# Two MLPs of a decoder trunk: up projections with activations held in the array, seven block products for eight in three of eight chunk pairs, and one written order for all engines

## The chip, the cores and the metric

The kernel runs on one core of one Trainium2 chip. Its metric is device microseconds of one execution; the number given for a kernel is the median over its runs. The engines of a core are named as in the profile: PE is the matrix engine (PEld its weight loads), DVE the vector engine, ACT the scalar engine, POOL and SP the two others. SP's queue issues the loads of weights.

## The reference, cut to what matters

D is 2048, there are 256 tokens (two blocks of 128, called b = 0 and 1 below), the hidden width of an MLP is 8192, and everything is float32.

```python
def sq_relu_mlp(u, w_up, w_down):
    return jnp.square(jax.nn.relu(u @ w_up)) @ w_down
...
    for i in range(DEPTH):
        u = rmsnorm(h, mix_pre_g[i])
        if i < N_A:
            m = short_conv_mixer(u, a_w_in[i], a_conv_w[i], a_w_out[i])
        else:
            j = i - N_A
            m = stick_breaking_mixer(u, b_w_q[j], k_sh, v_sh, b_w_o[j])
        h = h + rmsnorm(m, mix_post_g[i])
        u = rmsnorm(h, mlp_pre_g[i])
        h = h + rmsnorm(sq_relu_mlp(u, mlp_w_up[i], mlp_w_down[i]), mlp_post_g[i])
        if i == N_A - 1:
            kv = rmsnorm(h, kv_norm_g) @ w_kv
```

Layer 0 mixes with a gated convolution (a 2048 x 6144 and a 2048 x 2048 projection), layer 1 with causal stick-breaking attention over 16 heads (projections k, q, v and o of 2048 x 2048 each). Both layers end in an MLP of 2048 x 8192 and 8192 x 2048.

## The kernel before

**Numbers in two parts.** Each float32 operand is split into a high part (ACT copies it to the type fp32r, line 148) and a low part (DVE subtracts the high part, line 151). A product of two operands is three matmuls: high x high, high x low, low x high. Activations are split once; each weight is split once, in chunks of 128 x 1024 that SP loads into a ring of 4 buffers (`RAW`); the two parts go to a ring of 7 (`RING`).

**Stages, in order.** The projection into the convolution (lines 423 and 425), the projection out of it, the MLP of layer 0, the stage of k, q and v with the attention between them, the projection o, the MLP of layer 1.

**An MLP.** The hidden width is cut into four quarters of 2048. Each quarter is an up stage and then a down stage.
- *Up* (`up`, lines 550 and 557; 552 at the start of a layer): for each 128 x 128 tile of the weight, the tile is the held operand, and the activations stream past it: one matmul of 512 columns (the high tile against the high and the low part of 256 tokens) and one of 256 columns (the low tile against the high part). Eight tiles of a column go together. The result comes out transposed, features on the partitions, which is how the down stage wants it. `hidden` (lines 530 to 533) adds the two halves, applies the squared ReLU on DVE, and `split_tile` (176, 177) splits it.
- *Down* (`Group.half`, lines 224 to 226): the activations are the held operand, 128 x 128, and 512 columns of the weight stream: three matmuls of 512 columns, which I call a product. A quarter has two groups (`project`), one for each half of the 2048 output columns; a group has 16 chunks, and each chunk two token blocks and two halves of 512 columns: 64 products. Its four results, (b, c), are in four PSUM banks. Down results of the quarters are summed in SBUF (line 593).

**Norms.** `Norms.post` and `finish` (lines 301 to 334) take the last results of a stage, form the residual h, multiply it by the row of gains, and `enter` has PE transpose it (line 182), ACT and DVE split it (189, 190). At such a seam the last four chunks are done block by block (`EDGE`), so that block 0 is normalised while PE works on block 1.

**Who sets the order.** PE's order is written by hand. That of the other engines comes from the framework's scheduler, with some instructions marked as urgent, and small steps of the attention and the norms are put off by delays in a clock that counts PE's work (`at`, `spent`). h lives in SBUF throughout.

Of the kernel before, what the change touches and what calls it, by code (L numbers as in the profile page):

```python
# [2 lines left out]

# [12 lines left out]
P = 128  # L16
# [12 lines left out]
LEAD_UP = 6  # L29
ALONE = 8  # L30
RING = 7
RAW = 4
AHEAD = 4
CALM = 12
UNIT = 1.36
TURNS = (4.7, 6.8, 10.5, 13.0)
SQUARES = 20.0
TILE_HIGH = 0.227
TILE_LOW = 0.12
FIRST = 2  # L40
QUARTERS = FF // D

IN_N = [j * KD + i for i in range(KD) for j in range(3)]


def lead_then_rows(ns, lead):

    return [(k, n) for k in range(KD) for n in ns[:lead]] + [(k, n) for n in ns[lead:] for k in range(KD)]


IN_ORDER = lead_then_rows(IN_N, LEAD)
UP_FIRST = lead_then_rows(list(range(KD)), LEAD_UP)
UP_ORDER = lead_then_rows(list(range(KD)), 0)

G_MIX0, G_KV, G_MIX1, G_C0, G_C1, G_C2 = range(6)
B_POST0, B_MLP0, B_MPOST0, B_POST1, B_MLP1, B_MPOST1 = range(6)
# [3 lines left out]
def trunk(ctx, tc, x, xT, vecs, rows, ws, out):  # L60
    nc = tc.nc
    ctx.enter_context(tc.manual_schedule(engines={mybir.EngineType.PE}))
    const = ctx.enter_context(tc.tile_pool(name="const", bufs=1))
    stat = ctx.enter_context(tc.tile_pool(name="stat", bufs=8))
    res = ctx.enter_context(tc.tile_pool(name="res", bufs=8))
    act = ctx.enter_context(tc.tile_pool(name="act", bufs=8))
    wpool = ctx.enter_context(tc.tile_pool(name="w", bufs=RAW))
    wsplit = ctx.enter_context(tc.tile_pool(name="ws", bufs=RING))
    psum = ctx.enter_context(tc.tile_pool(name="ps", bufs=1, space=bass.MemoryType.PSUM))

    gv = const.tile([P, 6, KD], F32, name="gv")
    nc.scalar.dma_start(gv[:], vecs.rearrange("p (g k) -> p g k", g=6))

    def g(i, k):
        return gv[:, i, k : k + 1]

    eps = const.tile([P, 1], F32, name="eps")
    nc.vector.memset(eps[:], EPS)
    mean = const.tile([P, P], F32, name="mean")
    nc.vector.memset(mean[:], 1.0 / D)  # L80
    ones = const.tile([P, P], F32, name="ones")
    nc.vector.memset(ones[:], 1.0)

    def selected(name, pattern, op, multiplier):
        t = const.tile([P, P], F32, name=name)
        nc.gpsimd.affine_select(
            out=t[:], in_=ones[:], pattern=[[pattern, P]], compare_op=op,
            fill=0.0, base=0, channel_multiplier=multiplier,
        )
        return t  # L90

    later = selected("later", -1, ALU.is_gt, 1)
    causal = selected("causal", 1, ALU.is_gt, -1)
    ident = selected("ident", 1, ALU.is_equal, -1)
    later_r = const.tile([P, P], F32R, name="later_r")
    nc.vector.tensor_copy(later_r[:], later[:])
    ones_r = const.tile([P, P], F32R, name="ones_r")
    nc.vector.tensor_copy(ones_r[:], ones[:])
    nc.scalar.preload_act_table_set("sqrt_and_others")

    def bank(i, name):
        return psum.tile([P, 512], F32, tag=f"b{i}", name=name)


    stream = []

    class Weights:


        def __init__(self, ap, gains=None):  # L110
            self.ap, self.gains = ap, gains
            self.base = len(stream)
            stream.extend((self, c) for c in range(ap.shape[0]))

    raw, parts = {}, {}
    last_load = [None]
    count = {"loaded": 0, "split": 0, "limit": 1 << 30}
    gate = []

    def behind(kind):  # L120
        return tc.issue_after(gate[kind].ins) if gate else nullcontext()

    def load_one():
        i = count["loaded"]
        if i >= len(stream):
            return
        w, c = stream[i]
        t = wpool.tile([P, CW], F32, tag="raw", name=f"raw{i}")
        n = HALF if i < FIRST else CW
        for a in range(0, CW, n):  # L130
            last_load[0] = nc.sync.dma_start(t[:, a : a + n], w.ap[c, :, a : a + n])
        raw[i] = t
        count["loaded"] += 1

    def split_one():
        i = count["split"]
        while count["loaded"] <= i:
            load_one()
        w, c = stream[i]
        t = raw.pop(i)  # L140
        hi = wsplit.tile([P, CW], F32R, tag="hi", name=f"whi{i}")
        lo = wsplit.tile([P, CW], F32R, tag="lo", name=f"wlo{i}")
        gains = w.gains(c) if w.gains else [None] * (4 if i < FIRST else 1)
        n = CW // len(gains)
        for j, gain in enumerate(gains):
            at = slice(j * n, (j + 1) * n)
            with behind(0):
                nc.scalar.activation(hi[:, at], t[:, at], AF.Copy, scale=1.0 if gain is None else gain)  # L148
            with behind(1):
                if gain is None:  # L150
                    nc.vector.tensor_tensor(lo[:, at], t[:, at], hi[:, at].bitcast(F32), op=ALU.subtract)  # L151
                else:
                    nc.vector.scalar_tensor_tensor(  # L153
                        lo[:, at], t[:, at], gain, hi[:, at].bitcast(F32), op0=ALU.mult, op1=ALU.subtract
                    )
        parts[i] = hi, lo
        count["split"] += 1
        load_one()

    def chunk(i):  # L160
        while count["split"] <= min(i + (AHEAD if i >= CALM else 2), len(stream) - 1, max(i, count["limit"])):
            split_one()
        return parts[i]


    def operand(name):
        return act.tile([P, 4, 2, NB, P], F32R, tag="x4", name=name)

    def part_of(xs, k, b, i):
        return xs[k // 4][:, k % 4, i, b, :]  # L170

    def split_tile(xs, k, src):

        hi, lo = xs[k // 4][:, k % 4, 0, :, :], xs[k // 4][:, k % 4, 1, :, :]
        src = src.rearrange("p (b t) -> p b t", b=NB)
        nc.scalar.activation(hi, src, AF.Copy)
        nc.vector.tensor_tensor(lo, src, hi.bitcast(F32), op=ALU.subtract)

    def transposed(src, to):

        for j in range(4):
            nc.tensor.transpose(to[:, j * P : (j + 1) * P], src[:, j * P : (j + 1) * P], ident[:])  # L182
        return to[:].rearrange("p (k t) -> p k t", k=4)

    def operand_from(src, x4, b, to):
        t = transposed(src, to)
        hi, lo = x4[:, :, 0, b, :], x4[:, :, 1, b, :]
        return (
            nc.scalar.activation(hi, t, AF.Copy),
            nc.vector.tensor_tensor(lo, t, hi.bitcast(F32), op=ALU.subtract),  # L190
        )


    clock = {"us": 0.0, "seq": 0}
    due = []

    def at(delay, fn):
# [47 lines left out]
    def run(groups, enter=False, leave=False):  # L245
# [6 lines left out]
        for gr, i in units[first:last]:  # L252
            if i == 0 and gr.start is not None:
                gr.start()
            for b in range(NB):
                gr.unit(b, i)
# [595 lines left out]
```

## Time and profile before

| what | |
|---|---|
| median of 3 runs (lowest, highest) | 2197.94 us (2196.91, 2198.6) |
| the profiled execution: span from first to last instruction | 2195.9 us, 2.0 under the median |
| PE busy | 2171.5 us, 99% of the span, 11058 matmuls |
| DVE busy | 1334.1 us, 61% |
| ACT busy | 1115.9 us, 51% |
| moved by DMA | 417 MB, mean 190 GB/s |

The page's span is the profiled execution's own time as far as the profile shows it; what lies around it is the difference to the runs' times, some 2 us. A group of instructions is given as a line with its count, then busy time and the mean duration of one in ns, then the idle time of its engine just before its instructions and who ended it. Mean durations overlap on one engine: the next instruction often starts before the one ahead has ended, so what an instruction costs in a dense stretch is the distance between starts, which the timeline shows.

### The profile page before, as it was taken

To read this page: it belongs to the slowest core of one execution; us is meant where nothing else is said; L and a number is where in the kernel's file an instruction comes from. 1 tells how busy PE (TensorE), PEld (TensorE's weight loads), DVE (VectorE), ACT (ScalarE), POOL (GpSimd) and SP (SyncE) were. 2 spreads that over 40 slices of the span, in tenths; PEclk is the share of its full clock that TensorE was granted. 3 is DMA by queue.
4 is the path that set the end of the run, shared out by engine and by line. 5 is a ranking of instruction groups with operands and counts; after the bars stand their busy time and mean duration, and the time that the engine had idled before them with its cause. 6 is when DMAs were issued, how large, how long until landed. Compare 5 with 4: busy or idle time off the path is not lost.

```text
span 2195.9 us, 28873 instructions
## 1 busy us (share of the span) xinstructions
PE 2171.5 (99%) x11058; PEld 1852.0 (84%) x11058; DVE 1334.1 (61%) x1830; ACT 1115.9 (51%) x1534; POOL 4.3 (0%) x13
## 2 busy tenths in 40 slices
PE   8999999999999999999999999999999999999998
PEld 7888888888888888888788888879888888888886
DVE  7766656754654664565656777467545645655655
ACT  7544445544443443444557887455445434544443
POOL 0000000000000000000000000000000000000000
PEclk9999999999999999999999999999999999999999
DMA  8666565666656656655565556556666666666663
GB/s 304 205 191 188 188 229 163 211 190 193 193 185 195 193 185 193 194 188 180 175 201 163 157 160 195 188 173 203 189 193 192 186 194 195 187 189 198 186 190 115
DMA packets 114618, 417.16 MB, mean 190 GB/s; under 512 B 12849, under 2 KB 12849, under 8 KB 113457
## 3 DMA queue, kind: packets, MB, share of 16 engines
q1 hardware_dynamic: 112896, 407.95, 58.8%
q0 software_dynamic: 864, 6.29, 0.8%
q8 instruction: 86, 1.41, 0.2%
q10 hardware_dynamic: 720, 1.10, 0.1%
q14 instruction: 52, 0.42, 0.1%
HBM read 413.19 MB, written 2.10 MB: 189 GB/s over the span
## 4 chain that ended last, share of the span: by engine, by line
PE 97%; DVE 2%; ACT 0%; issue 0%; DMA 0%; DVEq 0%; ACTq 0%
PE up L550 20%; PE acc L224 17%; PE acc L226 17%; PE acc L225 17%; PE up L557 11%; PE acc L423 7%; PE acc L425 4%; PE lead L423 1%; DVE h L324 1%; PE tr L182 1%; PE up L552 1%; PE lead L425 1%; DVE hg L334 0%; PE z L645 0%; PE o L693 0%
## 5 line engine op out<-in xcount | busy, mean ns | idle before, releaser
L151 DVE TENSOR_TENSOR wlo<-raw,whi 128x1024 fp32r<-128x1024 f32 (+1 forms) x678 | 822.0, 1215 | 714.0 <-ACT whi L148 703.4
L148 ACT ACTIVATE whi<-raw 128x1024 fp32r<-128x1024 f32 (+1 forms) x678 | 712.5, 1053 | 932.3 <-PE acc L226 448.0
L550 PE MATMUL up<-u,whi 128*128 128x512 f32 x1952 | 489.4, 392 | 0.0
L550 PEld LDWEIGHTS up<-u,whi 128*128 128x128 f32 x1952 | 351.2, 189 | 62.8
L224 PE MATMUL acc<-whi,hid 128*128 128x512 f32 x1024 | 398.5, 389 | 0.0
L225 PE MATMUL acc<-wlo,hid 128*128 128x512 f32 x1024 | 398.4, 389 | 0.0
L226 PE MATMUL acc<-whi,hid 128*128 128x512 f32 x1024 | 398.4, 389 | 0.0
L557 PEld LDWEIGHTS up<-u,wlo 128*128 128x128 f32 x2048 | 278.6, 190 | 19.4
L557 PE MATMUL up<-u,wlo 128*128 128x256 f32 x2048 | 285.1, 282 | 0.0
L226 PEld LDWEIGHTS acc<-whi,hid 128*128 128x128 f32 x1024 | 192.3, 188 | 40.0
L224 PEld LDWEIGHTS acc<-whi,hid 128*128 128x128 f32 x1024 | 192.3, 188 | 39.6
L225 PEld LDWEIGHTS acc<-wlo,hid 128*128 128x128 f32 x1024 | 192.3, 188 | 39.4
L423 PE MATMUL acc<-u,whi 128*128 128x512 f32 x672 | 168.4, 392 | 0.0
L153 DVE SCALAR_TENSOR_TENSOR wlo<-raw,gv,whi 128x512 fp32r<-128x512 f32 (+1 forms) x160 | 132.2, 853 | 54.5 <-ACT whi L148 53.8
L224 PE MATMUL acc<-whi,u 128*128 128x512 f32 x384 | 153.2, 399 | 0.1
L226 PE MATMUL acc<-whi,u 128*128 128x512 f32 x384 | 150.0, 391 | 1.5 <-DVE u L190 1.5
L148 ACT ACTIVATE whi<-raw,gv 128x512 fp32r<-128x512 f32 (+1 forms) x160 | 121.9, 801 | 56.3 <-PE acc L226 49.7
L225 PE MATMUL acc<-wlo,u 128*128 128x512 f32 x384 | 149.7, 390 | 0.0
L423 PEld LDWEIGHTS acc<-u,whi 128*128 128x128 f32 x672 | 120.9, 189 | 21.6
L425 PEld LDWEIGHTS acc<-u,wlo 128*128 128x128 f32 x672 | 91.7, 190 | 6.6
L425 PE MATMUL acc<-u,wlo 128*128 128x256 f32 x672 | 93.7, 282 | 0.0
L226 PEld LDWEIGHTS acc<-whi,u 128*128 128x128 f32 x384 | 72.1, 188 | 17.5 <-DVE u L190 2.0
(133 smaller groups left out, 1607.4 us busy)
## 6 DMA issues: line engine op xcount, KB each, us to landing
raw<-w_up SPq DMA_DIRECT2D x256, 512.0 KB, 3.7
raw<-w_dn SPq DMA_DIRECT2D x256, 512.0 KB, 3.6
raw<-w_in SPq DMA_DIRECT2D x94, 512.0 KB, 4.4
raw<-w_out SPq DMA_DIRECT2D x32, 512.0 KB, 3.8
raw<-w_v SPq DMA_DIRECT2D x32, 512.0 KB, 4.3
raw<-w_k SPq DMA_DIRECT2D x32, 512.0 KB, 4.2
raw<-w_q SPq DMA_DIRECT2D x32, 512.0 KB, 3.9
raw<-w_wo SPq DMA_DIRECT2D x32, 512.0 KB, 4.3
```

Of the source, the lines that this page charges most:

```text
L148: nc.scalar.activation(hi[:, at], t[:, at], AF.Copy, scale=1.0 if gain is None else gain)
L151: nc.vector.tensor_tensor(lo[:, at], t[:, at], hi[:, at].bitcast(F32), op=ALU.subtract)
L153: nc.vector.scalar_tensor_tensor(lo[:, at], t[:, at], gain, hi[:, at].bitcast(F32), op0=ALU.mult, op1=ALU.subtract)
L182: nc.tensor.transpose(to[:, j * P : (j + 1) * P], src[:, j * P : (j + 1) * P], ident[:])
L224: nc.tensor.matmul(ps[:], xh, hi[:, a], start=i == 0 and k == 0, stop=False)
L225: nc.tensor.matmul(ps[:], xh, lo[:, a], start=False, stop=False)
L226: nc.tensor.matmul(ps[:], xl, hi[:, a], start=False, stop=i == self.n - 1 and k == self.ks - 1)
L324: nc.vector.scalar_tensor_tensor(piece(h[b], c), self.mg[b][c], r[:], piece(h[b], c), op0=ALU.mult, op1=ALU.add)
L423: nc.tensor.matmul(ps[:], w, xs, start=k == 0, stop=False)
L425: nc.tensor.matmul(ps[:, :T], w, xs[:, :T], start=False, stop=k == KD - 1)
L550: nc.tensor.matmul(ps, weight(0, k, n), x, start=k == 0, stop=False)
L557: nc.tensor.matmul(pss[n][:, :T], weight(1, k, n), x, start=False, stop=k == KD - 1)
```

## The change

Most of the file is written anew; the stages, the split into high and low parts and the chunks of 128 x 1024 stay. (Tile names: ru, hu, lu are a chunk of an up weight as loaded, its high and its low part, rd, hd, ld the same of a down weight; the digits are layer, quarter, group, chunk, or with a letter a to d the four operands of a seven.)

1. **Up with activations held.** Up stages now use the same three matmuls of 512 columns as the down stages (`product`, line 560): two groups of 64 products in a quarter. The result has tokens on the partitions, so each 128 x 512 result is evicted, transposed by PE in four 128 x 128 pieces, passed through ReLU and square on ACT, and split (`up_evict`). Before, hidden results needed no transposes.

2. **Seven products for eight.** A pair of chunks is a 2 x 2 block matrix of the weight (two k blocks, two halves of 512 columns) and meets a 2 x 2 block matrix of activations (two token blocks, two k blocks): eight products. In 14 of the 16 groups of an MLP, three of the eight pairs (`UP_SEVEN`, `DN_SEVEN`) take seven products of sums instead (`Group.seven`): DVE makes four sums of weight blocks of 512 columns (t1 to t4), which yields three and a half chunks to split in place of two; four sums of activation blocks are made once per operand (`make_forms`). Three of the seven products go into the accumulators of the group, four into banks q1, q5, q6 and q7, added up over the three pairs. After the third one, `combine` makes four sums of these on ACT and DVE, and the eviction adds one of them to each accumulator on DVE. The two groups without sevens are the first up and the last down group of an MLP. The order of pairs in a group is 3, 0, 4, 1, 5, 2, 6, 7, where 0, 1 and 2 are the sevens.

3. **One written order for all engines.** Nothing is left to the framework's scheduler. Every instruction is a task with a duration, buffers, PSUM banks and a due time; `Plan.place` walks through a model of the engines at build time, and the order that comes out is issued on all of them. Rings are now `SLOTS`: 8 for loaded chunks, 6 for high and 6 for low parts.

4. **Smaller.** Down results of quarters 1 to 3 start from the sum so far, which ACT copies into the PSUM bank (`seeds`). h goes to DRAM (`hs`) and comes back for the next norm. The gains ahead of an MLP are applied per feature during the split behind the transposes, no longer as a row.

```diff
-RING = 7
-RAW = 4
...
+SLOTS = {"raw": 8, "r2": 2, "hi": 6, "lo": 6, "x8": 8, "x4": 6, "c2": 14}
...
+UP_SEVEN = (0, 1, 2)
+DN_SEVEN = (0, 1, 2)
...
-                nc.tensor.matmul(ps, weight(0, k, n), x, start=k == 0, stop=False)
...
-                nc.tensor.matmul(pss[n][:, :T], weight(1, k, n), x, start=False, stop=k == KD - 1)
...
+    def product(ps, xh, xl, hi, lo, first, last, skip):
+        def fn():
+            for j, (a, w) in enumerate(((xh, hi), (xh, lo), (xl, hi))):
+                nc.tensor.matmul(
+                    ps.w(), a.w(), w.w(), start=first and j == 0, stop=last and j == 2, skip_group_check=skip
+                )
...
+        def seven(self, j, last):
...
+            b11, b22, b21, b12 = r0.col(0, HALF), r0.col(HALF, CW), r1.col(0, HALF), r1.col(HALF, CW)
+            t1, t2, t3, t4 = r2.col(0, HALF), r2.col(HALF, CW), b12, r3.col()
...
+                tt(t1, b12, b11, ALU.add)
+                tt(t3, b12, b22, ALU.add)
+            tt(t2, t1, b22, ALU.add)
+            tt(t4, t2, b21, ALU.add)
...
+            x2 = split(r2, f"{self.name}{j}c")
+            prod(q(5), "q5", s("s1"), x2, 0)
+            prod(q(6), "q6", s("s2"), x2, 1)
+            x0 = split(r0, f"{self.name}{j}a")
+            prod(q(1), "q1", a(0, 0), x0, 0)
+            prod(self.acc(0, 1).col(), (0, 1), s("s4"), x0, 1)
+            x1 = split(r1, f"{self.name}{j}b")
+            prod(q(7), "q7", s("s3"), x1, 1)
+            prod(self.acc(0, 0).col(), (0, 0), a(0, 1), x1, 0)
+            x3 = split(r3, f"{self.name}{j}d", 0, HALF)
+            prod(self.acc(1, 0).col(), (1, 0), a(1, 1), x3, 0)
...
+        def combine(self):
...
+            act(q1, q[1].col(), AF.Copy, soon=1.0)
+            tt(v, q[6].col(), q1, ALU.subtract, soon=2.0)
+            tt(v5, v, q[5].col(), ALU.add, soon=3.0)
+            tt(v, v, q[7].col(), ALU.add, soon=4.0)
+            tt(w5, v, q[5].col(), ALU.add, soon=5.0)
...
+                        st = add
+                        tt(st, ps, add, op, soon=1.5)
+                    tr = bank(banks[b][c], "tr")
+                    transposed(tr, st)
...
+                        act(r.col(), tr.col(), AF.Relu, soon=4.0)
+                        act(r.col(), r.col(), AF.Square, soon=8.0)
...
+                    act(piece(hid, n, 0, b), src, AF.Copy, soon=9.0)
+                    tt(piece(hid, n, 1, b), src, piece(hid, n, 0, b), ALU.subtract, soon=10.0)
```

**The order at three places.** All are in layer 0, third quarter. First PE in the second half of the up stage. Before, this is one column of 16 tiles (whi272 and whi273 are the high parts of two chunks, u4 the activations).

```order
L550 MATMUL up_6869<-u4_3416,whi272_6766 128x512 x4
L550 MATMUL up_6869<-u4_3477,whi272_6766 128x512 x4
L557 MATMUL up_6869<-u4_3416,wlo272_6767 128x256 x4
L557 MATMUL up_6869<-u4_3477,wlo272_6767 128x256 x4
L550 MATMUL up_6869<-u4_3547,whi273_6788 128x512 x4
L550 MATMUL up_6869<-u4_3589,whi273_6788 128x512 x4
L557 MATMUL up_6869<-u4_3547,wlo273_6789 128x256 x4
L557 MATMUL up_6869<-u4_3589,wlo273_6789 128x256 x4
```

Now it is pairs of chunks; these are the first four of the seven products of pair 0 in the second group (us0 holds the sums of activations, u0 the plain ones).

```order
L560 MATMUL q5_6756<-hu0210c_6646,us0_3537 128x512
L560 MATMUL q5_6756<-lu0210c_6658,us0_3537 128x512
L560 MATMUL q5_6756<-hu0210c_6646,us0_3537 128x512
L560 MATMUL q6_6761<-hu0210c_6646,us0_3537 128x512
L560 MATMUL q6_6761<-lu0210c_6658,us0_3537 128x512
L560 MATMUL q6_6761<-hu0210c_6646,us0_3537 128x512
L560 MATMUL q1_6769<-hu0210a_6656,u0_3250 128x512
L560 MATMUL q1_6769<-lu0210a_6696,u0_3250 128x512
L560 MATMUL q1_6769<-hu0210a_6656,u0_3250 128x512
L560 MATMUL acc01_6703<-hu0210a_6656,us0_3537 128x512
L560 MATMUL acc01_6703<-lu0210a_6696,us0_3537 128x512
L560 MATMUL acc01_6703<-hu0210a_6656,us0_3537 128x512
```

Matmuls of 256 columns are gone from the MLP, and two products in a row share a half or a whole of an operand that DVE has just made.

Second PE where this up stage ends and the down stage begins, before:

```order
L550 MATMUL up_7235<-u4_3547,whi287_7154 128x512 x4
L550 MATMUL up_7235<-u4_3589,whi287_7154 128x512 x4
L557 MATMUL up_7235<-u4_3547,wlo287_7155 128x256 x4
L557 MATMUL up_7235<-u4_3589,wlo287_7155 128x256 x4
L224 MATMUL acc00_7293<-whi288_7184,hid4_6501 128x512
L225 MATMUL acc00_7293<-wlo288_7185,hid4_6501 128x512
L226 MATMUL acc00_7293<-whi288_7184,hid4_6501 128x512
```

and now (tr is a transposed result, q0 to q3 the four evicted results, hid1 the hidden activations of an earlier group):

```order
L560 MATMUL acc11_6725<-hu02115_6995,u3_3519 128x512
L443 MATMUL tr_7077<-ident_72,q0_6976 128x128 x4
L443 MATMUL tr_7082<-ident_72,q2_7002 128x128 x4
L560 MATMUL acc00_7039<-hd0206_7007,hid1_6765 128x512
L560 MATMUL acc00_7039<-ld0206_7046,hid1_6765 128x512
L560 MATMUL acc00_7039<-hd0206_7007,hid1_6765 128x512
L443 MATMUL tr_7095<-ident_72,q1_6993 128x128 x4
L443 MATMUL tr_7103<-ident_72,q3_7025 128x128 x4
L560 MATMUL acc01_7015<-hd0206_7007,hid1_6765 128x512
```

Sixteen transposes have come in between the first products of the down stage.

Third DVE at the same seam, before (s and hid4 are the hidden results on their way, wlo288 the first low part of the down weights):

```order
L532 TENSOR_TENSOR s_7073<-up_7026,half_7071 128x256
L533 SCALAR_TENSOR_TENSOR s_7073<-s_7073 128x256
L151 TENSOR_TENSOR wlo287_7155<-raw287_7053,whi287_7154 128x1024
L177 TENSOR_TENSOR hid4_6919<-s_7073,hid4_6919 128x256
L151 TENSOR_TENSOR wlo288_7185<-raw288_7083,whi288_7184 128x1024
L532 TENSOR_TENSOR s_7125<-up_7078,half_7123 128x256
L533 SCALAR_TENSOR_TENSOR s_7125<-s_7125 128x256
L151 TENSOR_TENSOR wlo289_7207<-raw289_7105,whi289_7206 128x1024
```

and now, from the four evictions on:

```order
L397 TENSOR_TENSOR q0_6976<-acc00_6683,q0_6976 128x512
L397 TENSOR_TENSOR q2_7002<-acc01_6703,q2_7002 128x512
L397 TENSOR_TENSOR q1_6993<-acc10_6720,q1_6993 128x512
L397 TENSOR_TENSOR q3_7025<-acc11_6725,q3_7025 128x512
L397 TENSOR_TENSOR rd0200c_6982<-rd0200c_6982,rd0200a_6980 128x512
L397 TENSOR_TENSOR rd0200b_6981<-rd0200b_6981,rd0200a_6980 128x512
L397 TENSOR_TENSOR rd0200d_7113<-rd0200c_6982,rd0200b_6981 128x512
L397 TENSOR_TENSOR hid2_7100<-hid_7088,hid2_7100 128x4x128
L397 TENSOR_TENSOR ld0200c_7124<-rd0200c_6982,hd0200c_7111 128x1024
L397 TENSOR_TENSOR rd0201c_7066<-rd0201b_7065,rd0201a_7064 128x512
L397 TENSOR_TENSOR rd0201c_7066<-rd0201c_7066,rd0201a_7064 128x512
L397 TENSOR_TENSOR ld0200a_7150<-rd0200a_6980,hd0200a_7139 128x1024
```

The evictions stand at one place in DVE's row, ahead of the sums and the low parts for the first seven of the down group (rd0200, ld0200); what stands behind them includes the low parts of the hidden results (hid2).

More of the change, by code (lines that the diff above doesn't have):

```diff
@@ L92, in trunk @@
[L92 to L102, printed above, removed]
@@ L135, in split_one @@
[L135 to L158, printed above, removed]
@@ L179, in transposed @@
[L179 to L191, printed above, removed]
@@ L194, in trunk @@
[L194 to L216 removed]
+    pages = ctx.enter_context(tc.tile_pool(name="pages", bufs=1))
@@ L220, in half @@
+        def half(self, b, c, i, last):
+            hi, lo = self.parts(i)
+            ps = self.acc(b, c)
             for k in range(self.ks):
                 a = (k if self.ks == 2 else c) * HALF
[L222 to L225 removed]
@@ L245, in run, with unit @@
-    def run(groups, enter=False, leave=False):
-        units = [(gr, i) for gr in groups for i in range(gr.n)]
+                kk = i * self.ks + k
+                product(
+                    ps.col(), blk(self.X, kk, 0, b), blk(self.X, kk, 1, b), hi.col(a, a + HALF), lo.col(a, a + HALF),
+                    self.first((b, c)), last and k == self.ks - 1, self.seeds is not None or bool(self.sevens),
+                )
+        def unit(self, b, i, last=False):
+            for c in range(len(self.banks[b])):
+                self.half(b, c, i, last)
@@ L248, in run @@
+    def run(groups, enter=False, leave=False):
+        units = [(gr, i) for gr in groups for i in range(gr.n)] if (enter or leave) else []
+        if not units:
+            for gr in groups:
+                gr.whole()
+            return
         first, last = EDGE if enter else 0, len(units) - (EDGE if leave else 0)
@@ L616, in trunk @@
+    outs = two_groups("o", ws["out"], y, mix0)
+    outs[0].start = mix0.prepare
+    run(outs, leave=True)
+    mlp(0, mix0, kv)
     W3 = T + P
@@ new lines, in trunk, with tile_of @@
+    groups[-1].evict = keep_v1
+    side["set"] = 0
+    wos = two_groups("wo", ws["wo"], o, mix1)
+    wos[0].start = mix1.prepare
+    run(groups + wos, enter=True, leave=True)
+    mlp(1, mix1, end)
+    plan.settle()
+    plan.place()
+    table = [None]
+    def tile_of(b):
+        if b.tile is None:
+            if b.bank is not None:
+                b.tile = psum.tile(b.shape, b.dt, tag=f"b{b.bank}", name=b.name)
+            else:
+                b.tile = pages.tile(b.shape, b.dt, tag=f"{b.cls}{b.slot}", name=b.name)
```

1424 lines of the change are left out of this document (952 added, 472 removed).

## The prediction

> **What bounds the kernel now.** I read the page first, then the granted clock, then the busy time of the engines stage by stage, then the groups that give prices, then PE's and DVE's instructions in order of time. The page, with PE's row, and the chain that ended last by engine:
>
> ```profile
> span 2195.9 us, 28873 instructions
> PE 2171.5 (99%) x11058; PEld 1852.0 (84%) x11058; DVE 1334.1 (61%) x1830; ACT 1115.9 (51%) x1534; POOL 4.3 (0%) x13
> ...
> PE 97%; DVE 2%; ACT 0%; issue 0%; DMA 0%; DVEq 0%; ACTq 0%
> ```
>
> The chain is PE from end to end. The clock leaves nothing to win or lose:
>
> ```profile
> core 0: 2195.9 us, clock 0.999
> ```
>
> Busy time by stage: from:to, length, then PE, PEld, DVE, ACT, POOL, the clock, DMA's share and GB/s. The rows are the first up stage of layer 0, a down stage, an up stage, a down stage, the attention's stage, the projection o, and the tail after the last matmul's start.
>
> ```profile
> 365.37:461.82 96.45, 93.99 (x588) 84.45 (x589) 70.38 (x108) 55.39 (x91) 0.53 (x1) 1.00 0.62 197
> 461.82:548.89 87.07, 87.07 (x387) 72.11 (x385) 40.40 (x35) 37.46 (x41) 0.00 (x0) 1.00 0.61 192
> 548.89:638.25 89.36, 89.36 (x514) 78.66 (x512) 55.64 (x77) 44.75 (x65) 0.00 (x0) 1.00 0.61 190
> 638.25:725.31 87.06, 87.06 (x386) 72.10 (x385) 43.30 (x41) 33.96 (x34) 0.00 (x0) 1.00 0.61 192
> 1078.65:1380.28 301.63, 297.68 (x1389) 246.09 (x1388) 209.49 (x374) 231.45 (x353) 0.53 (x1) 1.00 0.55 175
> 1380.28:1473.96 93.68, 93.32 (x420) 77.19 (x420) 47.25 (x58) 41.33 (x58) 0.53 (x1) 1.00 0.56 179
> 2186.54:2195.90 9.36, 0.39 (x2) 0.00 (x0) 5.77 (x12) 1.11 (x3) 0.00 (x0) 0.66 0.51 196
> ```
>
> In the MLP's stages PE is busy all the time and DVE about half or two thirds. So a matmul removed there is worth its full distance to the next, as long as DVE, which gets the new work, keeps up. The whole question is the second half of that sentence.
>
> **Products removed.** A down stage is 128 products (two groups of 64) in 87.06 us: 0.680 us each. Sevens save one product per pair, three pairs in 14 groups of two MLPs: 84 products, 84 x 0.680 = 57.1 us off.
>
> **Up in the other form.** An up stage becomes 128 products as well: 89.36 - 87.06 = 2.30 us less in each of eight, 18.4 us off. The first up stage of a layer has 7.1 us more than a plain one, for transposes and waits at the seam; the new order crosses that seam with the same number of transposes, and I leave it as it is, 3 us either way per layer.
>
> **Transposes added.** PE around one group of four in the attention's stage (start, length):
>
> ```profile
> 1198.61 0.39 PE L226 MATMUL acc<-whi,u 128*128 128x512 f32 x1
> 1198.84 0.60 PE L182 MATMUL tr<-ident,tk 128*128 128x128 f32 x4
> 1199.19 0.48 PE L224 MATMUL acc<-whi,u 128*128 128x512 f32 x1
> 1199.51 0.39 PE L225 MATMUL acc<-wlo,u 128*128 128x512 f32 x1
> ```
>
> From the start of L226 to that of L225 are 0.90 us, in which two matmuls alone take 0.680 x 2/3 = 0.45: four transposes cost 0.45 us. Sixteen up groups with four results each make 64 such fours: 64 x 0.445 = 28.5 us on. Their whole duration is another matter:
>
> ```profile
> L182 PE MATMUL tr<-ident,tk 128*128 128x128 f32 x64 | 9.6, 272 | 0.0
> ```
>
> 272 ns each, but 0.445 / 4 = 0.111 us of PE's time. The Trainium skill's page "TensorE: Matmul & The Clock Gate", Part 4, gives about 275 ns for a transpose in a kernel's context; charged for each of 256, this is an estimate by that page of 70 us for this term, and the sum would come out 42 us later. The trace agrees with the page on the duration, and its starts speak against charging it.
>
> **Other stages.** Convolution, attention and o keep their matmuls. Their orders are new, but DVE (209 of 302 us) and ACT (231) have room there; I put them at nothing, 3 us either way. The tail of 9.36 us is a chain of DVE and ACT behind the last matmul; one addition leaves it and one pair of squares moves into it, so nothing, 1 us either way. Loads are as many, over a shorter time: DMA's share would go from 0.61 to some 0.64.
>
> **DVE's bill.** Prices (mean durations in ns), and three neighbours in time:
>
> ```profile
> L151 DVE TENSOR_TENSOR wlo<-raw,whi 128x1024 fp32r<-128x1024 f32 x670 | 819.1, 1224 | 714.0 <-ACT whi L148 703.4 <-PE up L557 7.6 <-PE lead L425 1.9
> L593 DVE TENSOR_TENSOR mg<-mg,acc 128x512 f32<-128x512 f32 x48 | 31.1, 682 | 19.9 <-PE acc L226 19.6
> L177 DVE TENSOR_TENSOR hid<-s,hid 128x256 fp32r<-128x256 f32 x128 | 53.0, 419 | 4.0 <-ACT hid L176 3.9
> L684 DVE TENSOR_TENSOR lb<-lb,ey 128x128 f32<-128x128 f32 x32 | 8.9, 280 | 0.5 <-PE ey L681 0.5
> ```
>
> ```profile
> 599.48 1.23 DVE L151 TENSOR_TENSOR wlo<-raw,whi 128x1024 fp32r<-128x1024 f32 x1 [1.23 <-ACT whi L148]
> 600.62 0.42 DVE L532 TENSOR_TENSOR s<-up,half 128x256 f32<-128x256 f32 x1
> 601.07 0.42 DVE L533 SCALAR_TENSOR_TENSOR s<-s 128x256 f32<-128x256 f32 x1
> ```
>
> An instruction that doesn't need the one ahead starts 1.14 us after a subtraction of 1024 (0.08 before its end); one that does starts 0.03 after the end. So I count 1.14 for 1024 columns, 0.60 for 512 (0.72 if it depends), 0.34 for 256, 0.20 for 128. A seven costs DVE three and a half chunks and four sums: 3 x 1.14 + 0.60 + 2.6 = 6.6 us, while PE takes 7 x 0.680 = 4.8. A plain pair costs it 2.3 against PE's 5.4. A group with three sevens and five plain pairs: 31.2 us, with `combine` (four dependent sums, 2.9) and the evictions (four, 2.4) 36.5. The second up group also has the low parts of four hidden results (2.4) and the forms for the down stage (ten of 256, four of 128: 4.2): 43.1. The first down group has four low parts: 38.9. PE for the four groups of a quarter: 61 x 0.680 = 41.5, twice with 1.8 for transposes:
>
> up 0: DVE 36.5, PE 41.5; up 1: 43.1 and 43.3; down 0: 38.9 and 43.3; down 1: 36.5 and 41.5.
>
> DVE comes to 155 of PE's 170 us. PE stays the bound in the sum, but in the second up group only just. ACT is far from it:
>
> ```profile
> L148 ACT ACTIVATE whi<-raw 128x1024 fp32r<-128x1024 f32 x670 | 709.8, 1060 | 932.3 <-PE acc L226 448.0 <-PE up L550 303.3 <-PE acc L423 77.1
> L189 ACT ACTIVATE u<-tr 128x512 fp32r<-128x512 f32 x24 | 13.8, 585 | 7.1 <-PE tr L182 7.1
> ```
>
> 19 chunks and three halves at 1.06 and 0.59, twelve steps on hidden results at 0.59 and six forms make some 32 us in the second up group, of 43.
>
> **Waits that the written order adds.** At a seam DVE waits for the group's last products before it can evict, and what stands behind it in its row, the low parts for the next seven, waits too. The trace shows such a wait (PE's matmul, DVE's addition, DVE's next low part):
>
> ```profile
> 899.48 0.39 PE L226 MATMUL acc<-whi,hid 128*128 128x512 f32 x1
> ...
> 899.90 0.69 DVE L593 TENSOR_TENSOR mg<-mg,acc 128x512 f32<-128x512 f32 x1 [1.08 <-PE acc L226]
> ...
> 900.51 1.22 DVE L151 TENSOR_TENSOR wlo<-raw,whi 128x1024 fp32r<-128x1024 f32 x1
> ```
>
> DVE stood for 1.08 us at the head of its row, started 0.42 us after the start of the matmul that it waited for, and the low part behind it came after that. The Trainium skill's page "PSUM — Partial Sum Buffer", section "Engine vs sequencer instructions", says that the queues of ScalarE and VectorE are strict first in, first out; the row agrees.
>
> I walk through the seam up to down of the order shown above, with time 0 where PE can start the next matmul, 0.23 us after the last one's start. The last eviction starts at 0.2 by the rows above, and all end by about 1.0. Then two sums (1.2), a dependent one (0.7), one low part of a hidden result (0.6) and the low part of c (1.14) end at 4.65; PE needs it after eight products and sixteen transposes, 8 x 0.680 + 1.78 = 7.2. Two more sums and a: 7.1, needed at 8.6. b: 8.3, needed at 9.9. A sum and d: 9.5, needed at 11.3. A sum and the next chunk: 11.3, needed at 12.0. Three hidden low parts and a chunk: 14.2, needed at 14.7. From there on the lead grows again. So the smallest lead is 0.5 us; likewise some 1.3 us ahead of the third seven of the second up group. What delays DVE by more than that (a late high part from ACT, a page not yet free) PE waits for. From below it is nothing, since the walk comes out; from above it is that wait of 1.08 us, passed on to PE at each of 32 seams, 35 us. I take 0.5 us at two of the four seams of each of eight quarters, 8 us, near the lower end because the walk has no negative lead.
>
> **Sum.** 2195.9 - 57.1 - 18.4 + 28.5 + 8 = 2156.9 us for the span, and 2.0 more for the median of the runs: **2159 us**.
>
> **Rivals.**
>
> *DVE sets the pace (0.14).* If sums of weight blocks don't overlap, full durations count: the second up group then costs 5 x 2.45 + 3 x (3 x 1.224 + 5 x 0.682) + 12 x 0.682 + 10 x 0.419 + 4 x 0.280 = 47.0, 3.7 over PE, the other groups stay under theirs. 8 x 3.7 = 30 us in place of the 8: 2181. For it: in those steps each sum needs the one ahead. Against it: the starts quoted.
>
> *The written order stalls at every seam (0.08), slower.* DVE reaches the evictions early and stands, as in the row above; behind it the next low parts come late, and PE starts each group with a wait. Without stalls the median would be 2151; the point from which it decides is 51 us over 32 seams, 1.6 us each. At 2 us it gives 2151 + 64 = 2215. For it: leads of 0.5 us in the walk. Against it: two chunks of low parts stand ahead of the evictions and give PE 7.2 us of cover.
>
> *Transposes cost their duration (0.03).* 256 x (0.272 - 0.111) = 41 us on top: 2200, no change that can be told.
>
> *The gain leaks away in small waits outside the MLPs (0.03)*, some 40 us over the attention and the three norms: 2199, likewise.
>
> *It doesn't do what it says (0.02).* The written order has all products of the sevens, so I see no way but waits, 2150 to 2200.
>
> **How the numbers follow.** The likeliest case (0.70) is PE's sum with 0 to 20 us of waits. The measurement of this kernel can tell about 0.2%, 4.4 us. Faster by more than that takes the likeliest case, DVE's pace and most of the last: 0.88. Within it: 0.04. Slower: 0.08. The range goes from 2146 (no waits, 5 us won at the seams and in the other stages) to 2188 (35 us of waits and 2 for the other stages).
>
> **What would show it.** A full quarter should take 170 to 171 us where it took 176.4 (89.36 + 87.06). A down stage of quarters 1 and 2 should have 122 products; DVE should be busy for 75% or more of the span with PE's waits for its low parts under 20 us in sum. If PE waits for L397 several us at each seam, the second rival holds; if it waits in the second up group alone, the first. I am wrong if the sum of PE's waits in the MLPs is over 35 us, or if products there take other than 0.680 us.

## The result, and the profile after

The changed kernel takes **2144.11 us** (median of 4 runs, 2143.97 to 2144.65), against 2197.82 of the kernel before on the same chip: a ratio of **0.9755, 95% interval 0.9742 to 0.9768**, 53.7 us less. The forecast was 2159, with a range from 2146 to 2188. The direction was right, the gain 15 us larger than forecast, and the time lies 2 us below the range. Of all runs here one, of the kernel with three additions in experiment 1, was slow (3060 us at a granted clock of 0.654) and is left out of the ratios.

The page of the changed kernel:

```profile
span 2142.5 us, 27458 instructions
PE 2121.9 (99%) x9942; PEld 1773.0 (83%) x9942; DVE 1725.9 (81%) x2325; ACT 1283.8 (60%) x1787; POOL 1.0 (0%) x7
...
PE 99%; ACT 0%; DVE 0%; DMA 0%; issue 0%; DVEq 0%; ACTq 0%
```

The span is 53.4 us shorter. DVE went from 61% to 81%, and it is still PE alone that sets the end. Busy time by stage, with the columns as before: the first up stage of layer 0 and of layer 1, an up and a down stage (quarter 1 of layer 0), the attention, the projection o.

```profile
366.52:460.73 94.21, 92.54 (x424) 76.27 (x423) 80.32 (x129) 63.88 (x113) 0.00 (x0) 0.98 0.56 185
1445.65:1538.26 92.61, 90.94 (x424) 75.09 (x423) 80.30 (x130) 63.89 (x113) 0.00 (x0) 1.00 0.58 188
545.14:630.70 85.56, 85.56 (x391) 71.06 (x390) 78.34 (x101) 50.45 (x66) 0.00 (x0) 1.00 0.59 195
630.70:714.67 83.97, 83.97 (x378) 69.64 (x377) 78.22 (x92) 53.65 (x65) 0.00 (x0) 1.00 0.63 202
...
1056.65:1352.88 296.23, 296.20 (x1385) 245.97 (x1384) 208.75 (x372) 207.55 (x332) 0.00 (x0) 1.00 0.56 184
1352.88:1445.65 92.77, 92.77 (x421) 77.29 (x420) 48.46 (x57) 41.96 (x58) 0.00 (x0) 1.00 0.59 195
```

In the up, the down and the o stage the length and PE's busy time are the same to the hundredth. A full quarter takes 85.56 + 83.97 = 169.5 us, and 244 products of 0.680 with eight fours of transposes at 0.445 are 165.9 + 3.6 = 169.5: nothing is left for waits. The attention's stage, which had 4 us of idle PE, has 0.03.

**Where the 53.4 us went.** By stages of the two traces: the two MLPs together took 713.3 + 721.9 = 1435.2 us and now take 690.1 + 696.9 = 1387.0, 48.2 less; the attention 5.4 less, o 0.9 less, and the start and the convolution with its projection 1.2 more. (Of the attention's 5.4, some 0.45 is a four of transposes that PE now does ahead of the stage's start, in the MLP before it.) Without its term for waits the forecast had 57.1 + 18.4 - 28.5 = 47.0 for the MLPs. So the terms that count instructions are right within 1.2 us in sum, and the miss of 14.4 us in the span is 8 us of waits that never came, 5.1 us net in stages that I had put at nothing, and this 1.2.

What PE waits for, all rows of the view over 1 us; ahead of the colon the engine, the tile and line, and whom it waited for, behind it the us in total, the times and the longest. Before:

```profile
PE lead L423 <- ACT whi L148: 5.9, 1, 5.9
PE tr L182 <- DVE hg L334: 2.3, 2, 1.2
PE up L552 <- DVE u L190: 2.3, 4, 0.8
PE acc L226 <- DVE u L190: 1.5, 1, 1.5
PE ey L681 <- DVE kT L715: 1.3, 3, 0.4
```

After:

```profile
PE lead L436 <- ACT hin L389: 6.9, 1, 6.9
PE tr L443 <- ACT relu L389: 2.0, 2, 1.0
PE q L560 <- ACT hid L389: 1.4, 2, 0.7
PE lead L436 <- DVE u L404: 1.3, 1, 1.3
```

No low part of a weight stands in the list after. The waits of the norms' seams (hg and u) and of the attention (u, kT) are gone; new ones behind ACT's ReLU have come, at one place of each layer, and one of 1.3 us for u in the projection into the convolution.

### The profile page after: what moved, and what is told of

Read it like the earlier page. It is cut to its first block, busy times and chain, and to the rows that moved or that the text cites. A ratio compares the mean times of both kernels' runs of the same rounds, so it can differ in the third digit from the quotient of the medians.

```text
span 2142.5 us, 27458 instructions
## 1 busy us (share of the span) xinstructions
PE 2121.9 (99%) x9942; PEld 1773.0 (83%) x9942; DVE 1725.9 (81%) x2325; ACT 1283.8 (60%) x1787; POOL 1.0 (0%) x7
## 4 chain that ended last, share of the span: by engine, by line
PE 99%; ACT 0%; DVE 0%; DMA 0%; issue 0%; DVEq 0%; ACTq 0%
PE acc L560 72%; PE acc L436 11%; PE q L560 11%; PE tr L443 2%; PE lead L436 2%; PE z L1193 0%; PE o L1243 0%; PE ex L1223 0%; PE o L1244 0%; PE z L1194 0%; DMA x<-xT 0%; ACT hid L389 0%; ACT hu L389 0%; DVE hh L404 0%; PE ey L1228 0%
## 5 line engine op out<-in xcount | busy, mean ns | idle before, releaser
L560 PE MATMUL acc<-hu,u 128*128 128x512 f32 x1376 | 439.7, 391 | 0.0
L560 PE MATMUL acc<-hd,hid 128*128 128x512 f32 x1376 | 435.4, 390 | 0.0
L560 PEld LDWEIGHTS acc<-hd,hid 128*128 128x128 f32 x1376 | 258.4, 188 | 53.0
L560 PEld LDWEIGHTS acc<-hu,u 128*128 128x128 f32 x1376 | 258.3, 188 | 52.7
L560 PE MATMUL acc<-lu,u 128*128 128x512 f32 x688 | 267.8, 389 | 0.0
L560 PE MATMUL acc<-ld,hid 128*128 128x512 f32 x688 | 267.8, 389 | 0.0
L397 DVE TENSOR_TENSOR ld<-rd,hd 128x1024 fp32r<-128x1024 f32 x172 | 208.1, 1222 | 51.3 <-ACT hd L389 49.7
L397 DVE TENSOR_TENSOR lu<-ru,hu 128x1024 fp32r<-128x1024 f32 x172 | 208.4, 1222 | 42.6 <-ACT hu L389 41.4
L389 ACT ACTIVATE hd<-rd 128x1024 fp32r<-128x1024 f32 x172 | 180.1, 1057 | 101.9 <-PE acc L560 73.8
L389 ACT ACTIVATE hu<-ru 128x1024 fp32r<-128x1024 f32 x172 | 178.8, 1059 | 84.3 <-PE acc L560 55.1
```

What stands on the lines that cost most here:

```text
L389: nc.scalar.activation(out_.w(), in_.r(), func, scale=val(scale), **more)
L397: "DVE", dve(width(out_)), lambda: nc.vector.tensor_tensor(out_.w(), a.r(), b.r(), op=op),
L560: nc.tensor.matmul(ps.w(), a.w(), w.w(), start=first and j == 0, stop=last and j == 2, skip_group_check=skip)
```

## The experiments

Ratios are to the kernel before on the same chip, with 95% intervals.

**1. How much lead DVE has at the seam.** Scratch additions behind the last eviction of each up stage; every other instruction keeps its place.

```diff
+            nc.vector.tensor_tensor(out_.w(), a.r(), b.r(), op=op)
+            for _ in range(n):
+                nc.vector.tensor_tensor(pad.tile[:], ones.tile[:], ones.tile[:], op=ALU.add)
...
-                        tt(st, ps, add, op, soon=1.5)
+                        if (j, b, c) == (1, 1, 1):
+                            delayed(st, ps, add, op, 3)
+                        else:
+                            tt(st, ps, add, op, soon=1.5)
```

With three:

> The changed kernel with three additions of 128 columns (0.20 us each from start to start, 0.6 us together, on a scratch tile) right behind DVE's last eviction at each of the eight seams from up to down; everything else is issued in the same order. Theory A (DVE has a lead at the seam, 0.68 us at its smallest by the changed kernel's trace, and PE doesn't wait): nothing is seen, 2143 to 2145.5 us. Theory B (the seam is already tight, as the forecast's 8 us had it): 8 x 0.6 = 4.8 us more, 2149.

Measured: 2143.86 us, 0.9754 (0.9741 to 0.9768). Nothing is seen; in its trace the up stage of quarter 1 is 85.56 us long as before, the down stage 83.99 to 83.97. With twelve:

> The same with twelve additions at each seam, 2.4 us. Theory A: what goes beyond the smallest lead of about 0.7 us is passed on to PE, 8 x (2.4 - 0.7) = 13.6 us: 2158 us, between 2155 and 2160, and PE waits behind the low parts of the third hidden result or of the first plain chunk of the down group. Theory B (no lead): 8 x 2.4 = 19 us, 2163. Theory C (the leads are much larger than the trace's distance between a low part's end and its first use says, or DVE's idle time swallows it): 2144 to 2147.

Measured: 2159.55 us, 0.9827 (0.9814 to 0.9841), 15.4 us more than the changed kernel. First the seam in the changed kernel itself; time 0 of the walk is where PE's transposes start, 629.91. PE:

```profile
629.68 0.39 PE L560 MATMUL acc<-hu,u 128*128 128x512 f32 x1
629.91 1.03 PE L443 MATMUL tr<-ident,q 128*128 128x128 f32 x8
...
644.85 0.39 PE L560 MATMUL acc<-ld,hid 128*128 128x512 f32 x1
```

and DVE:

```profile
633.46 1.23 DVE L397 TENSOR_TENSOR ld0100c<-rd0100c,hd0100c 128x1024 fp32r<-128x1024 f32 x1 [0.26 <-ACT hd0100c L389]
634.60 0.68 DVE L397 TENSOR_TENSOR rd0101c<-rd0101b,rd0101a 128x512 f32<-128x512 f32 x1
635.32 0.69 DVE L397 TENSOR_TENSOR rd0101c<-rd0101c,rd0101a 128x512 f32<-128x512 f32 x1
635.93 1.22 DVE L397 TENSOR_TENSOR ld0100a<-rd0100a,hd0100a 128x1024 fp32r<-128x1024 f32 x1
637.07 1.22 DVE L397 TENSOR_TENSOR ld0100b<-rd0100b,hd0100b 128x1024 fp32r<-128x1024 f32 x1
...
642.95 1.22 DVE L397 TENSOR_TENSOR ld<-rd,hd 128x1024 fp32r<-128x1024 f32 x1
```

The walk had c ready at 4.65, a at 7.1, b at 8.3 and the chunk behind the third hidden low part at 14.2; the rows give 4.78, 7.24, 8.38 and 14.26. That last one ends at 644.17, and PE first uses it at 644.85: a lead of 0.68 us, the smallest of all chunks in the MLPs of this trace, where the walk had 0.5 at the same chunk. With three additions DVE has, around the same chunk:

```profile
630.12 0.93 DVE L735 TENSOR_TENSOR pad<-ones 128x128 f32<-128x128 f32 x3
...
642.86 1.21 DVE L397 TENSOR_TENSOR ld<-rd,hd 128x1024 fp32r<-128x1024 f32 x1
```

and PE, in the same kernel:

```profile
644.25 0.39 PE L560 MATMUL acc<-ld,hid 128*128 128x512 f32 x1
```

The chunk ends at 644.07, 0.18 us ahead of its use. The additions moved DVE by 0.85 us, not 0.6 (each writes the tile that the one ahead writes, and takes about 0.3 us). 0.34 of it went into the wait for ACT in the row of ld0100c (0.26 of idle time, and the 0.08 by which a row can start ahead of the end of the one before); the rest, 0.50, came out of the lead. With twelve, DVE and then PE:

```profile
630.14 3.87 DVE L735 TENSOR_TENSOR pad<-ones 128x128 f32<-128x128 f32 x12
...
637.60 0.50 PE L560 MATMUL q<-ld0100c,hs 128*128 128x512 f32 x1 [0.65 <-DVE ld0100c L397]
640.07 0.50 PE L560 MATMUL q<-ld0100a,hid 128*128 128x512 f32 x1 [0.80 <-DVE ld0100a L397]
644.14 0.50 PE L560 MATMUL acc<-ld,hid 128*128 128x512 f32 x1 [0.40 <-DVE ld L397]
```

DVE is moved by 3.8 us. Less the 0.34 and the 0.63 of lead that can be used (PE starts 0.05 us behind a low part's end here) 2.8 are left, and that down stage is 2.97 us longer. The three idle times in the rows make only 1.85 us: the view counts them from the modelled end of a matmul, some 0.39 us after its start, while without a wait the next starts after 0.23, and the matmul behind a stop takes 0.33 to the next. A stop so costs PE more than the idle time shown. Quarters 1 and 2 behave so in both layers; the last down stage of each grew by 2.3, and the first not at all, where the low parts have leads of over 4 us in the changed kernel's trace. These six stages make 16.5 us; the span grew by 15.9, since the start took 1.0 more and the first up stage of layer 0 took 1.6 less (the last section says why). So Theory A stands: the leads are real, they end where the walk said, and what exceeds them goes to PE.

**2. What the sevens are worth.** `UP_SEVEN` and `DN_SEVEN` empty:

```diff
-UP_SEVEN = (0, 1, 2)
-DN_SEVEN = (0, 1, 2)
+UP_SEVEN = ()
+DN_SEVEN = ()
```

> The changed kernel with no sevens: every group takes eight products per pair, and the sums, the combining and the forms go. Theory A (PE's starts set the time, and the sevens give their products and nothing else): 84 products of 0.680 us come back, 2144.1 + 57.1 = 2201.2 us, between 2198 and 2204, and a full quarter takes 256 x 0.680 + 8 x 0.445 = 177.6 us where it took 169.5. Theory B (the sevens make DVE hold PE up somewhere that the profile doesn't show, so that they are worth less than their products): under 2196. Theory C (the written order by itself brings much of the gain in the MLPs): under 2190.

Measured: 2205.95 us, 1.0034 (1.0021 to 1.0048): slower than the kernel before, and 61.8 us over the changed one, 4.7 more than 84 products. An up and a down stage:

```profile
552.35:641.68 89.33, 89.33 (x405) 73.94 (x404) 41.99 (x36) 43.71 (x53) 0.00 (x0) 1.00 0.62 189
641.68:730.30 88.62, 88.62 (x400) 73.34 (x398) 42.00 (x36) 44.97 (x54) 0.00 (x0) 1.00 0.62 190
```

A full quarter takes 177.95 us where 177.6 was expected. More than half of the 4.7 lies elsewhere, in the first up stages: this kernel's order has a wait at each layer's entry that the changed kernel doesn't have, with slow matmuls behind it:

```profile
370.00 1.22 PE L560 MATMUL acc<-hu,u 128*128 128x512 f32 x2 [2.45 <-DVE u L404]
371.02 0.63 PE L560 MATMUL acc<-lu,u 128*128 128x512 f32 x1
```

The time lies 2 us above the range of Theory A, and Theories B and C are refuted: the sevens give at least their products. They bring more than the whole gain; everything else in the change, the new form of up with its transposes and the written order above all, loses 8 us without them. What the written order alone is worth no run here separates.

**3. The price of a transpose.** Each hidden result is transposed twice, 64 fours more:

```diff
                     transposed(tr, st)
+                    transposed(tr, st)
```

> The changed kernel with the transposes of the hidden results issued twice, 64 fours more into the same banks. Theory A (a four costs PE the 0.445 us between starts): 28.5 us more, 2172.6 us, between 2170 and 2175, the seven up groups of a full quarter 1.78 us longer each. Theory B (they cost their duration, 0.272 us each): 256 x 0.272 = 70 us more, 2214. Theory C (part of them hides behind weight loads or waits): under 2168.

Measured: 2171.38 us, 0.9881 (0.9867 to 0.9894), 27.3 us more: 0.43 us a four, as Theory A had it. Their duration in that kernel is what it was:

```profile
L443 PE MATMUL tr<-ident,q 128*128 128x128 f32 x448 | 54.7, 272 | 0.0
```

The third rival, 272 ns each, would have been 70 us. The Trainium skill's page "TensorE: Matmul & The Clock Gate", Part 4, has about 275 ns, and the durations agree; but the run shows that a row of them costs PE 0.107 us each.

**4. Where DVE becomes the bound.** Four sevens in each of the 28 groups:

```diff
-UP_SEVEN = (0, 1, 2)
-DN_SEVEN = (0, 1, 2)
+UP_SEVEN = (0, 1, 2, 3)
+DN_SEVEN = (0, 1, 2, 3)
```

> The changed kernel with four sevens in place of three in each of the 28 groups (pair 3 as well, order of pairs 4, 0, 5, 1, 6, 2, 3, 7; two more pages for the forms, paid for with one of 8 buffers for loaded chunks and two of 14 temporary pages). PE has 28 products less, 19.0 us; a fourth seven costs DVE 6.6 - 2.3 = 4.3 us per group and 1.3 us more forms per quarter. Theory A (the DVE bill of the prediction is right, so DVE now sets the pace): 155 + 4 x 4.3 + 1.3 = 173.5 us of DVE against 166.8 of PE in a full quarter, so that a full quarter takes about 173.5 us where it took 169.5, and the others some 3 us more: 2172 us, between 2155 and 2180, and PE waits for DVE in the second up group above all. Theory B (DVE has far more room than the bill says, since PE waited for nothing with three): PE's sum alone, 2144.1 - 19.0 = 2125 us.

Measured: 2181.81 us, 0.9927 (0.9913 to 0.9940): 37.7 us slower than three, with 19 us less of products. Up and down of quarter 1, and two rows of PE's waits:

```profile
541.91:634.87 92.96, 88.60 (x393) 71.44 (x392) 89.94 (x119) 57.67 (x79) 0.00 (x0) 0.98 0.55 181
634.87:717.00 82.13, 82.02 (x361) 67.61 (x361) 81.63 (x99) 51.36 (x63) 0.00 (x0) 1.00 0.62 205
```

```profile
PE acc L560 <- ACT hid L389: 6.7, 8, 0.8
PE q L560 <- DVE lu0112a L397: 2.8, 1, 2.8
```

A quarter takes 175.1 us where the bill had 173.5, in the up stage, where DVE is busy for 89.94 of 92.96 us; each second up group of quarters 1 to 3 waits 2.8 us at its third seven. Quarters 1 and 2 take 175.1 us in both layers. The bill is right on who becomes the bound and where, and 1.6 us a quarter too low; the whole time lies 2 us above Theory A's range. Not foreseen were eight waits for ACT of 0.8 us each, where a down stage begins; the edit also takes a buffer for loaded chunks and two temporary pages away, and no run separates what that costs. One in the first up group of quarters 1 to 3 alone:

```diff
-        return UP_SEVEN if (q, j) != (0, 0) else ()
+        return () if (q, j) == (0, 0) else UP_SEVEN + (3,) if j == 0 else UP_SEVEN
```

> The fourth seven in the first up group of quarters 1 to 3 alone, where the bill leaves DVE 5 us (36.5 of 41.5): 6 groups, 6 products less; the forms of the fourth pair are made once per MLP; one page more for them, two of 14 temporary pages less. Theory A (the bill holds: DVE 40.8, PE 40.8 in that group, and the lead of some us that DVE brings along covers it): 6 x 0.680 = 4.1 us less, 2140 us, between 2139 and 2142. Theory B (the group is now tight and hands its lead of about 0.7 us at the later seams on as waits): 2144 or more.

Measured: 2150.62 us, 0.9782 (0.9768 to 0.9795), 6.5 us slower than the changed kernel. My theory fell. PE now stands in the next group, at the third seven of the second up group. The up stage of quarter 1, and the stop:

```profile
545.56:632.00 86.44, 85.52 (x389) 70.40 (x387) 82.26 (x107) 51.48 (x68) 0.00 (x0) 1.00 0.57 194
```

```profile
616.64 0.50 PE L560 MATMUL q<-lu0112a,u 128*128 128x512 f32 x1 [0.84 <-DVE lu0112a L397]
```

An up stage takes 86.44 us in place of 85.56, though it has a product less: 1.56 us are lost in each of six, of which 0.92 show as idle time. I had looked at the group that got the work (40.8 of 40.8) and not at the one behind it, which lives on the lead that this group hands over: the low part waited for has a lead of 2.33 us in the changed kernel's trace, and none here. The two groups together need 83.9 of DVE by the bill and have 84.1 of PE.

**5. The stop behind ACT's ReLU.** In the changed kernel PE stands at the end of the first up group of each layer. PE, then ACT:

```profile
421.94 0.66 PE L443 MATMUL tr<-ident,relu 128*128 128x128 f32 x4 [0.98 <-ACT relu L389]
423.28 0.66 PE L560 MATMUL q<-hu0010c,us 128*128 128x512 f32 x1 [0.69 <-ACT hid L389]
423.74 0.63 PE L560 MATMUL q<-lu0010c,us 128*128 128x512 f32 x1
```

```profile
419.86 1.06 ACT L389 ACTIVATE hu<-ru 128x1024 fp32r<-128x1024 f32 x1 [0.65 <-PE acc L560]
420.82 0.58 ACT L389 ACTIVATE hid<-tr 128x512 f32<-128x512 f32 x1
421.30 0.59 ACT L389 ACTIVATE relu<-acc 128x512 f32<-128x512 f32 x1
```

The ReLU stands behind a chunk's high part and another step in ACT's row. DVE can do it:

```diff
-                        act(st.col(), ps, AF.Relu, soon=1.5)
+                        ts(st.col(), ps, 0.0, None, ALU.max, soon=0.5)
```

It was tried on the kernel with the fourth seven in the first up group,

> The kernel before this one, with the first ReLU of the first up group of each layer on DVE (tensor_scalar with max) in place of ACT. In the changed kernel's trace PE stands there twice per layer, 1.38 us for a transpose behind ACT's ReLU and 0.96 us for a bank, in which 0.34 us are work, and in layer 0 the next matmuls run at 0.43 us a step. Theory A (these are waits for ACT, whose row has a split chunk ahead of the ReLU): about 2 us less per layer, 2136 us, between 2134 and 2138.5. Theory B (DVE is as late there as ACT): as the kernel before this one, within 1 us.

Measured: 2145.57 us, 0.9760 (0.9747 to 0.9774), 5.1 us less than without it. The range was missed because it started from the 2140 us expected of that kernel, which took 2150.62; of the difference, some 4 us were expected. Then on the changed kernel:

> The changed kernel with the first ReLU of the first up group of each layer on DVE in place of ACT, and nothing else. Theory A (the two stops of PE behind ACT there cost some 2 us per layer, and in layer 0 slower matmuls behind them): as between the two kernels with four sevens in the first up group, 5 us less, 2139 us, between 2138 and 2141. Theory B (what it brought there came from room that three sevens leave anyway): 2143 or more.

Measured: **2139.85 us, 0.9737 (0.9723 to 0.9750)**, 4.3 us less. The wait for the ReLU is gone from PE's list, of the one for the bank 1.0 us is left in two. The first up stages take 90.90 and 90.87 us where they took 94.21 and 92.61.

**6. A fourth seven where a roomy group follows.** With the ReLU on DVE:

```diff
-        return DN_SEVEN if (q, j) != (QUARTERS - 1, 1) else ()
+        return () if (q, j) == (QUARTERS - 1, 1) else DN_SEVEN + (3,) if j == 1 else DN_SEVEN
```

> That kernel with a fourth seven in the second down group of quarters 0 to 2 (6 products less), which is followed by the group with the most room (first up, 36.5 of 41.5 by the bill), not by the one with the least. The forms of pair 3 cost DVE 1.3 us more, in the second up group at the earliest, where the third seven's low parts have a lead of 1.96 us in the changed kernel's trace. One page more for the forms, two of 14 temporary pages less. Theory A (what decides is the lead at the third seven of the second up group, and 1.3 us don't use it up): 6 x 0.680 = 4.1 us less than without it, 2135 us, between 2134 and 2137. Theory B (any further DVE work in a quarter comes back as waits, as with the fourth seven in the first up group): as without it or more, 2139 to 2145.

Measured: **2136.40 us, 0.9719 (0.9705 to 0.9732)**, the fastest here, 61.9 us under the kernel before. Up and down of quarter 1, then the low part for the third seven, and PE's use of it:

```profile
541.17:626.79 85.62, 85.62 (x391) 71.08 (x390) 81.31 (x106) 52.59 (x71) 0.00 (x0) 1.00 0.58 197
626.79:710.06 83.27, 83.27 (x374) 69.07 (x373) 78.61 (x94) 53.03 (x65) 0.00 (x0) 1.00 0.61 202
```

```profile
611.84 1.22 DVE L397 TENSOR_TENSOR lu0112b<-ru0112b,hu0112b 128x1024 fp32r<-128x1024 f32 x1
```

```profile
613.26 0.40 PE L560 MATMUL q<-lu0112b,us 128*128 128x512 f32 x1
```

168.89 us, one product (0.64) less and no wait. The lead there is down from 1.96 us in the changed kernel to 613.26 - 613.06 = 0.2, 1.8 us less where 1.3 was expected. By this, a further DVE step of 0.3 us in the second up group would be paid for; that was not tried.

**7. The attention's waits.** Two attempts on the kernel before, each with one delay altered.

```diff
-            each(8.0, weights, a - 1)
+            each(9.4, weights, a - 1)
```

> The kernel before the change, with one delay of the attention altered: the weights of the former pair of heads are due 9.4 us of PE's work after q, not 8.0, so that they no longer stand right behind the transposes whose copy by DVE frees their PSUM bank. Theory A (three of the 301.6 us stage's waits, 0.71 us from ex to ey in place of 0.11, come from that copy): 3 x 0.6 = 1.8 us less in the stage, 299.8 us, and the whole 2196.0 us. Theory B (the time was lost to something else in the stage): the stage stays at 301.6 us.

Measured: 2202.96 us, 1.0024 (1.0015 to 1.0032), the stage 306.96 us. The wait for kT fell from 1.3 to 0.8 us, and a new one of 4.5 came. Then the other end, `at(1.9, turn)` in place of `at(3.0, turn)`:

> The kernel before the change, with the other end moved: the transposes of q and k are due 1.9 us of PE's work after their group, not 3.0, so that DVE's copy is done when the weights come; the weights' own delay stays at 8.0. Theory A (three waits of 0.6 us for that copy can be had by themselves): 1.8 us less in the attention's stage, 2196.0 us. Theory B (in this kernel each step moved puts another one in the way, as the weights moved later did): the stage at 301.6 us or more, 2197 to 2203.

Measured: 2199.56 us, 1.0004 (0.9996 to 1.0013), the stage 302.55 us. The largest wait of PE in that stage, of the first attempt and of the second:

```profile
PE ex L676 <- DVE lb L683: 4.5, 3, 1.8
```

```profile
PE tr L182 <- ACT tk L710: 2.7, 4, 0.7
```

In the second the wait for kT is gone and one for ACT's eviction of k and q has come. Both show that the waits in this stage are for such small steps, and neither of the two moves saved time: a new wait came each time. The written order has none of them, but the changed kernel differs in more than its order, and no run takes that apart.

## Why the prediction was right, and where it failed

- *What bounds the kernel: PE, as long as DVE keeps up.* Right. DVE's bill of 155 us a quarter stands against 78.34 + 78.22 = 156.6 busy.
- *Products removed, up in the other form, transposes added.* Right: 47.0 us in sum for the MLPs, 48.2 measured. A full quarter should lose 6.90 us by these terms and lost 6.89; 57.1 for the products is borne out by the full quarter without sevens, 0.445 a four by 0.43. The first up stages, by the same terms 96.45 - 2.30 - 3 x 0.680 + 1.78 = 93.9 us, took 94.21 and 92.61, and that was luck: the waits at the entry went (2.5 us of idle time in each), and the stop behind ACT's ReLU came in their place (1.7 in each, and in layer 0 another 1.6 of slow matmuls).
- ***Waits that the written order adds.*** **This step failed: 8 us were taken, and in the full quarters none came.** The walk beneath it was good to 0.2 us at each chunk, and it came out with positive leads everywhere. I then put 0.5 us on two of four seams for steps that might be late, bounded from above by a wait that the order of before had. None was late: the smallest lead measured is 0.68 us. The walk's own answer was zero, and experiment 1 shows that the lead it found is what DVE can be moved by before PE notices.
- ***Other stages.*** **This term was mis-sized: nothing was put for them, 5.1 us less came.** The rows that I quoted had 301.63 us against 297.68 of busy PE in the attention's stage, 4 us of waits that an order for all engines could remove, and I spoke only of how much room DVE and ACT have there. They have room on average; the small steps came late one by one. The changed stage has no idle PE; its other 1.5 us are the four transposes that moved ahead of it, and for the rest fit what a stop costs beyond its idle time. That it is the written order which removed these waits is likely, not shown.
- *The range* began at 2146, for no waits and 5 us won at the seams and in the other stages. From 2159 these are 13 us; just that came, and 2144.1 is what it gives with the last 1.2 us of the MLPs and 0.4 less around the span. The case that came true stood at the edge of the range. In the chances, 0.70 and 0.14 and most of 0.02 make at most 0.86, not 0.88.
- *The rivals.* DVE sets the pace: not with three sevens, where low parts and sums overlapped as counted (0.60 us from start to start, 0.72 for the dependent one in the rows of experiment 1), but with four it does. The written order stalls at every seam: no; its mechanism is real once DVE is late by more than its lead of 0.7 us. Transposes at their duration: refuted. The gain leaks away outside the MLPs: it went the other way.

## What to carry to other kernels

When DVE feeds PE, don't compare sums: walk along the written order through the tightest group and take the leads that come out as the answer, without a surcharge for what can't be named. Work added to DVE was paid here not in the group that got it but at the next place with the smallest lead, so put it where a roomy group follows. And a stage whose PE is idle for a few us with room on all engines is worth looking at step by step: here just those 4 us went with the new order.

## What the runs showed of the hardware that was not expected

A stop of PE can have slow matmuls behind it. Behind the stop of experiment 5 the matmuls in layer 0 of the changed kernel ran at half the clock, and those behind the same stop in layer 1 did not (the two stretches of 3.4 us behind it):

```profile
423.30:426.70 3.40, 3.40 (x8) 2.69 (x9) 2.52 (x6) 2.27 (x4) 0.00 (x0) 0.52 0.00 0
1502.40:1505.80 3.40, 3.40 (x15) 2.81 (x16) 2.83 (x7) 3.30 (x6) 0.00 (x0) 1.00 0.00 0
```

In 3.4 us 8 matmuls started in place of 15, at a granted clock of 0.52: some 1.6 us on top of the 1.7 us of waits, and the first up stage of layer 0 is 94.21 us to 92.61 of layer 1. The two waits of 2.45 us in the kernel without sevens both had the same behind them, 0.43 us from one matmul to the next.

This is not a property of the order. The same pair of stops, 0.98 and 0.69 us, stands in both layers of five kernels here: the changed one, the two with additions, and those with four sevens in all groups and in the first up group. In three of these ten places the clock fell to 0.50 for 3.41 us. In the kernel with twelve additions it fell in neither layer, and the first up stage of layer 0 took 92.63 us. Where DVE sets the pace a slow stretch cost nothing: with four sevens in all groups quarter 1 of layer 0 has one and quarter 2 has none, and both take 175.1 us.

The Trainium skill's page "TensorE: Matmul & The Clock Gate", Part 1, has the clock halved after an idle window of about 3.4 us, and says that the window runs freely, so that one kernel has different numbers of slow matmuls at its start from run to run. Three of ten like places agree with a free window. The stops here, 0.98 and 0.69 us with transposes between them and 2.45 us in one, were shorter than that window, and there the measurement decides.
